# RWKV chain: one prepared matrix per chunk, one product per head, output by tokens

## The chip, the cores and the metric

The kernel is one program on one core of a Trainium2 chip, written in Bass with the Tile framework. The metric is device time in microseconds (us). A core has TensorE (matrix products), VectorE, ScalarE and GpSimd (elementwise work), and SyncE, which issues the DMAs here; the profile calls them PE, DVE, ACT, POOL and SP, and TensorE's weight loads PEld.

## The reference

Two layers over 1024 latent tokens and 128 context tokens, 1024 channels. Layer 1's mixer runs a bidirectional RWKV-7 recurrence (512 channels, 8 heads of 64) beside a bidirectional mLSTM (the other 512). The change is in the recurrence, which for each head and direction carries a 64 x 64 state over the tokens:

```
def step(S, inp):
    r_t, w_t, k_t, v_t, kk_t, a_t = inp
    sa = einsum('bhvk,bhk->bhv', S, -kk_t)
    S = S * w_t[..., None, :] + sa[..., None] * (kk_t * a_t)[..., None, :] + v_t[..., None] * k_t[..., None, :]
    y = einsum('bhvk,bhk->bhv', S, r_t)
    return S, y
```

After the scan the outputs of both directions are added, normalised per head (`head_layer_norm`), and joined with a bonus term and a gate. The last states of the context tokens are outputs too.

## The kernel before

The tokens are columns and the channels partitions everywhere but in the recurrence, which is done in chunks of 64 tokens. A *step* is a pair of heads `p` (four pairs) and an index `i`: for `i` from 0 to 7 the 128-token block `i` forward and block `7 - i` backward, for `i = 8` the context block. A step thus has four units `u` (two directions, two chunks each) and two heads `hh` in the two halves of the partitions. There are 36 steps.

`odd_layer_mixer` sets the order of the work. Its `while` loop is a planner; a turn of it advances the chain of the current step by two stages (`chain_block`), each of at most two preparations by one (`prep`), a finished block by one (`finish`), and hands out pieces of other work by a quota: `R1` pieces a turn while the input projection is being made (`input_pieces`: large products of 384 tokens, L234 to L236), `R2` once the mLSTM runs. A new preparation starts at the earliest `STAG` turns after the last. The framework's scheduler then fixes each engine's order, mixing the pieces finely. Each engine runs its list in order.

`prep` is independent of the state, and has 19 stages. It loads `AG`, `BK` and `vv`; multiplies a chunk with itself (L1119) and masks that into `GB` and the other half of `AG` (L1122, L1123); transposes `BK` into `BT` (L1128); inverts a triangular 64 x 64 matrix per head in half precision, by merging blocks of 1, 2, .. 32 (L1149, L1166, L1171, L1086) and a Newton step (L1197 to L1202); and ends in `Pm` (L1207). `XV` and `UV` hold, for a head, the state or `U` in one half of the partitions and the values in the other.

`chain` depends on the state and is the recurrence from chunk to chunk. For a direction and a chunk it makes five products for each of two heads: `pr` from `AG` and `XV` (L1259), which VectorE copies to `rh`; `pu` from `Pm` and `rh` (L1267), copied to `UV`; `px` from `BT` and `UV` (L1272); and `py` as a sum of two products (L1274, L1275). ScalarE makes `Xw`, the decayed state (L1264); VectorE writes the new state; `py`, by channels, goes into `yo`. `finish` transposes `yo` to tokens for the norm (L1306) and back (L1320).

In the profile a float32 product leaves two MATMUL records, a transpose or a float32r or half-precision product one. `64*128` is the block of the array that a product uses: rows, then columns.

Of the kernel before, what the change touches and what calls it, by code (L numbers as in the profile page):

```python
# [12 lines left out]
F32 = mybir.dt.float32  # L13
# [4 lines left out]
OP = mybir.AluOpType  # L18
# [4 lines left out]
P = 128  # L23
# [28 lines left out]
# arrays of per-channel parameters, and their numbers of columns  # L52
# [11 lines left out]
def trunk_kernel(ctx: ExitStack, tc: tile.TileContext, A, outs, dbg=None, upto=99, odd="rm"):  # L64
    """A: input APs by name; outs: output APs; tokens are columns, channels are partitions."""
# [93 lines left out]
    def mod_ve(l, i0, pool, bank):  # L159
        """512 columns with the products on the vector engine, and only the last sum on the tensor engine."""  # L160
# [28 lines left out]
    def side(gens):  # L189
        """Steps of the generators in turn; a function that does the next n (a fraction: now and then one)."""  # L190
# [38 lines left out]
    def gemm(ps, W, cols, act, nk, start=True, stop=True):  # L229
        """ps += W[:, :, cols]^T act in three passes; act(part, k): the high or the low part of a k tile."""  # L230
# [10 lines left out]
    def rsqrt_small(dst, v, n, pool):  # L241
        """dst = v ** -0.5 on a small tile: a first value from the bits, then three Newton steps."""
# [9 lines left out]
    class Rms:  # L252
        """1 / rms of the tokens of x; the squares are added up tile by tile."""
# [14 lines left out]
        def cols(self, tb):  # L268
            """Tokens on partitions: [128, 3]."""
# [16 lines left out]
        def rows(self, tb, bank=None, r=None):  # L286
            """Repeated over the partitions (in PSUM): [128, 384]."""
# [12 lines left out]
    def norm_coef(l, which, k0=0, n=KT):  # L300
        """norm_w * (1 + scale) per stream: [128, 8, 2], or some of its tiles."""
# [10 lines left out]
    def new_h():  # L312
        """The high and low parts of 1024 channels: h(part, k, tb) is [128, 384]."""
# [35 lines left out]
    def accumulate_x(x, ps, l, which, m, tb):  # L349
        """x[tb][:, m] += gate * ps."""  # L350
# [5 lines left out]
    def mlp(x, l, h, last, add, after, later=()):  # L356
        """x += g2 * (relu(h @ w1)^2 @ w2), 512 hidden channels at a time."""
        with ExitStack() as es:
# [4 lines left out]
            def up(m, n=2.2):  # L363
                """A generator, a token block at a time."""
# [22 lines left out]
            # the first tiles on all but the last block, whose activations come last  # L387
# [21 lines left out]
            # the last hidden channels: a token block after another, half of the weights where the last block's  # L409
            # activations were  # L410
# [12 lines left out]
    def finish(x, tb, rms):  # L423
        """Final norm of a token block. A generator of four steps."""
# [66 lines left out]
            # shift and scale of the first norm  # L491
# [30 lines left out]
    # =========================== layer 0, mixer ===========================  # L522
    def norm(x, l, which):
        """The normalised activations; what takes in a tile of x; what computes a block of tokens."""
# [4 lines left out]
        def block(tb):  # L529
            """A generator of four steps."""  # L530
# [15 lines left out]
    def early(block):  # L546
        """A step of blocks 0 and 1 after each tile of the last block's products."""
        return itertools.chain(block(0), block(1))

    def even_layer_mixer(h, even_u, even_gate, zs, load_y):  # L550
        """Its output, split; what the tiles of channels come to in order."""
        yh = new_h()
        with ExitStack() as es:
# [4 lines left out]
            # block-diagonal gate weights: [128, (dir, which, tile), 128]  # L558
# [5 lines left out]
            # log_a / 4 and log_a / 2 at an open gate  # L564
# [9 lines left out]
            def rglru(j, u, gate):  # L574
# [11 lines left out]
                for d in range(2):  # L586
# [3 lines left out]
                    # sigmoid(x) = (1 + tanh(x / 2)) / 2  # L590
# [1290 lines left out]
```

## Time and profile before

| | before |
|---|---|
| device time, three runs | 3512.77, 3525.55, 3534.02 us (median 3525.55) |
| profiled execution, span | 3541.4 us |
| TensorE, VectorE, ScalarE busy in it | 3362.6, 1993.8, 1476.1 us |
| layer 1's mixer, first to last product | 1303.4 to 2607.4 us |
| TensorE busy there, mean granted clock | 1220.2 us of 1304.0, 0.90 |

The page gives no other time of the profiled execution than its span, from the first to the last instruction. Busy times count an engine's own instructions. A matmul's length includes its way through the array, so that neighbours overlap; what one costs is read from start to start. The granted clock is the share of TensorE's 2.4 GHz that it was given.

### The profile page before, as it was taken

How to read it: one execution, taken by the hardware profiler on the slowest of the kernel's cores; microseconds unless marked ns; L12 is line 12 of the kernel's file. 1: busy time of each engine (PE TensorE's matmuls, PEld its weight loads, DVE VectorE, ACT ScalarE, POOL GpSimd, SP SyncE). 2: the span in 40 equal slices, each digit the busy share in tenths (PEclk: the TensorE clock that was granted, in tenths of full speed). 3: DMA queues.
4: the chain of work that ended last, by engine and by line, in shares of the span. 5: the costliest groups of instructions: out<-in, count | busy, mean ns of one | idle time of the engine just before them, and what ended most of it. 6: DMA issues, size and time to landing. Idle time of an engine off the chain costs nothing. (4 is left out here: it accounts for less than half of the span.)

```text
span 3541.4 us, 57533 instructions
## 1 busy us (share of the span) xinstructions
PE 3362.6 (95%) x22456; PEld 3021.0 (85%) x22456; DVE 1993.8 (56%) x4326; ACT 1476.1 (42%) x3443; POOL 850.2 (24%) x709
## 2 busy tenths in 40 slices
PE   7887999999999998999999999998889999999998
PEld 4766999999999987777777677777789999999998
DVE  6786665555533375676576775647756333333335
ACT  4534332111122255655666566677845122221112
POOL 2232321112111233141151421113313111111112
PEclk9998999999999998888889899999989999999999
DMA  5334412322211125232132322246452111111111
GB/s 207 103 129 155 137 52 92 96 87 92 78 42 42 55 102 156 79 112 73 53 118 83 113 69 82 72 119 170 122 168 63 48 42 42 42 42 42 42 42 73
DMA packets 212978, 313.21 MB, mean 88 GB/s; under 512 B 38034, under 2 KB 154978, under 8 KB 211170
## 3 DMA queue, kind: packets, MB, share of 16 engines
q1 hardware_dynamic: 212706, 309.53, 27.6%
q8 instruction: 177, 2.90, 0.3%
q14 instruction: 95, 0.78, 0.1%
HBM read 250.72 MB, written 58.74 MB: 87 GB/s over the span
## 5 line engine op out<-in xcount | busy, mean ns | idle before, releaser
L234 PE MATMUL mm<-h,w 128*128 128x384 f32 x2552 | 903.6, 355 | 2.1 <-ACT h L503 1.2
L235 PE MATMUL mm<-h,w 128*128 128x384 f32 x2552 | 902.0, 353 | 3.0 <-POOL h L506 1.5
L236 PE MATMUL mm<-h,w 128*128 128x384 f32 x2552 | 900.3, 353 | 2.0 <-POOL w L217 2.0
L217 POOL TENSOR_TENSOR w<-w 128x1024 fp32r<-128x1024 f32 x153 | 373.6, 2442 | 1361.1 <-ACT w L216 1312.5
L216 ACT CAST w<-w 128x1024 fp32r<-128x1024 f32 x211 | 221.2, 1050 | 886.4 <-PE mm L235 769.8
L354 DVE SCALAR_TENSOR_TENSOR x<-mm,mod,x 128x384 f32<-128x384 f32 (+1 forms) x576 | 282.9, 514 | 444.8 <-PE mm L236 418.4
L234 PE MATMUL mm<-uH,w 128*128 128x384 f32 x1536 | 520.3, 339 | 0.0
L235 PE MATMUL mm<-uL,w 128*128 128x384 f32 x1536 | 519.2, 338 | 0.0
L236 PE MATMUL mm<-uH,w 128*128 128x384 f32 x1536 | 519.0, 338 | 0.0
L234 PEld LDWEIGHTS mm<-h,w 128*128 128x128 f32 x2552 | 493.9, 194 | 23.3 <-issue 11.3
L235 PEld LDWEIGHTS mm<-h,w 128*128 128x128 f32 x2552 | 493.6, 193 | 19.2 <-POOL h L506 4.5
L236 PEld LDWEIGHTS mm<-h,w 128*128 128x128 f32 x2552 | 494.4, 194 | 14.5 <-issue 4.5
L374 DVE SCALAR_TENSOR_TENSOR s<-mm,r 128x384 f32<-128x384 f32 x192 | 106.8, 557 | 405.6 <-ACT r L372 405.5
L234 PEld LDWEIGHTS mm<-uH,w 128*128 128x128 f32 x1536 | 288.7, 188 | 2.5 <-issue 2.5
L235 PEld LDWEIGHTS mm<-uL,w 128*128 128x128 f32 x1536 | 288.6, 188 | 0.0
L236 PEld LDWEIGHTS mm<-uH,w 128*128 128x128 f32 x1536 | 288.6, 188 | 0.0
L372 ACT ACTIVATE r<-mm 128x384 f32<-128x384 f32 x192 | 93.5, 488 | 276.9 <-PE mm L236 276.2
L217 DVE TENSOR_TENSOR uL<-s,uH 128x384 fp32r<-128x384 f32 x192 | 150.2, 783 | 87.6 <-ACT uH L216 87.2
L1086 ACT COPY DB<-YQ 64x256 f16<-64x256 f16 x360 | 144.4, 402 | 55.2 <-DVE YQ L1171 36.6
L1171 DVE CAST_PREDICATED YQ<-lm,sm 128x512 f16<-128x512 uint16 x180 | 123.6, 687 | 69.2 <-PE sm L1149 48.1
L1149 PEld LDWEIGHTS <-DB 128*128 128x128 f16 x1728 | 90.2, 101 | 83.2 <-issue 40.5
L216 ACT CAST uH<-s 128x384 fp32r<-128x384 f32 x192 | 98.5, 513 | 143.7 <-DVE s L374 143.5
(378 smaller groups left out, 5312.1 us busy)
## 6 DMA issues: line engine op xcount, KB each, us to landing
w<-in_mlp_w_dram SPq DMA_DIRECT2D x128, 512.0 KB
wmod<-in_w_mod_dram SPq DMA_DIRECT2D x80, 512.0 KB
w<-in_od_w_in_dram SPq DMA_DIRECT2D x31, 512.0 KB
w<-in_od_w_out_dram SPq DMA_DIRECT2D x24, 512.0 KB
zar<-AR SPq DMA_DIRECT2D x24, 384.0 KB
AG<-zar SPq DMA_DIRECT2D x144, 64.0 KB
BK<-zbk SPq DMA_DIRECT2D x72, 128.0 KB
hbig<-zm SPq DMA_DIRECT2D x18, 512.0 KB
```

Source lines behind the costliest of these rows:

```text
L216: sc.copy(Hout, src)
L217: eng.tensor_tensor(Lout, src, Hout.bitcast(F32), op=OP.subtract)
L234: te.matmul(ps, wH[:, k, cols], aH, start=start and k == 0, stop=False)
L235: te.matmul(ps, wH[:, k, cols], aL, start=False, stop=False)
L236: te.matmul(ps, wL[:, k, cols], aH, start=False, stop=stop and k == nk - 1)
L354: ve.scalar_tensor_tensor(xs, ps[:, o], modcol(l, 2 if which == 1 else 5, m, s), xs, op0=OP.mult, op1=OP.add)
L372: sc.activation(r, ps[:, :TB], AF.Relu)
L374: ve.scalar_tensor_tensor(s, ps[:, :TB], 0.0, r, op0=OP.max, op1=OP.mult)
L1086: sc.copy(dst[hr, :, hr], src[hr])
L1149: te.matmul(o[r_, u], lt[r_, u], rt[r_] if rt is i16 else rt[r_, u], start=True, stop=True)
L1171: ve.copy_predicated(YQ.rearrange("p w (d c) n -> p (w d) c n", d=2), lmask(l, 0, 4), pyq.rearrange("p (w c) n -> p w c n", c=2),)
```

## The change

For each unit and head the preparation now makes one 128 x 128 matrix, `EF`, that takes state and values (`XV`) to the new state before its decay and to the chunk's output, together. `prep` gets four more stages (23): it transposes the masked half of `AG` into `AT`, multiplies it with the inverse (`PD`, both heads on a diagonal) into `WT`, multiplies that with `GB` (which now also holds the transposed `BK`) and adds `AG`, in which an identity stands for the state's own part. `AG` becomes two fixed buffers, one for each of the two preparations under way, instead of three in turn.

`chain_block` then has one product per direction and head; VectorE multiplies the state's half with the decay `wend` into the next `XV`, and the other half is the output, already by tokens, in `ys`. Copies through `rh`, `UV`, `Xw` and `BT` go. `finish` needs no transpose before the norm, and four small products per block instead of one transpose behind it. `wend` is stored in the order of the chain; `AR` is stored to DRAM by three DMAs instead of one; the first states are loaded into `XV`. The planner's numbers change.

```
-        STAG = 10
-        R1, R2 = 0.32, 1.6
+        STAG = 11
+        R1, R2 = 0.29, 1.45
 # expand
-                    sy.dma_start(
-                        zar[p][d][:, tb * NC6 : tb * NC6 + NC6, :], AR.rearrange("p c a t -> p c (a t)")
-                    )
+                    sy.dma_start(zar[p][d][HR[1], cs6, :], AR[HR[1]].rearrange("p c a t -> p c (a t)"))
+                    for i in range(2):
+                        sy.dma_start(zar[p][d][HR[0], cs6, (1 - i) * CH : (2 - i) * CH], AR[HR[0], :, i])
 # prep
-            B.AG = mp.tile([P, 2, 4, P], F32, tag="AG", name="AG", bufs=NB)
+            AG = AGs[bank]
...
-            sc.copy(B.BT, pt.rearrange("p (u n) -> p u n", u=4))
+            ptv = pt.rearrange("p (u n) -> p u n", u=4)
+            for hh, hr in enumerate(HR):
+                ho = HR[1 - hh]
+                sc.copy(GB[hr, :, BETA[hh]], ptv[hr, :, hr])
+                sc.copy(AG[ho, :, 5 * hh], ptv[ho, :, hr])
...
+            pt = smps(bank)
+            for u in range(4):
+                te.transpose(pt[:, u * P : u * P + P], AG[:, u, 2:4].rearrange("p w n -> p (w n)"), ident)
+            AT = mp.tile([P, 4, P], F32, tag="AT", name="AT", bufs=1)
+            sc.copy(AT, pt.rearrange("p (u n) -> p u n", u=4))
+            yield
             pq = quads(smps(bank))
             mm2(pq, N1, Q)
-            B.Pm = mp.tile(U4, F32, tag="Pm", name="Pm", bufs=2)
-            ve.tensor_tensor(B.Pm, pq, Q, op=OP.add)
+            for hr in HR:
+                ve.tensor_tensor(PD[hr, :, hr], pq[hr], Q[hr], op=OP.add)
             yield
+            pw = smps(bank)
+            for u in range(4):
+                te.matmul(pw[:, u * P : u * P + P], PD[:, u], AT[:, u], start=True, stop=True)
+            WT = mp.tile([P, 4, P], F32, tag="WT", name="WT", bufs=1)
+            sc.copy(WT, pw.rearrange("p (u n) -> p u n", u=4))
+            yield
+            B.EF = mp.tile([P, 2, 4, P], F32, tag="EF", name="EF", bufs=2)
+            for hh, hr in enumerate(HR):
+                pf = smps(bank)
+                right = cols(GB, hh, EFFECT)
+                for u in range(4):
+                    te.matmul(pf[:, u * P : u * P + P], WT[hr, u], right[hr, u], start=True, stop=True)
+                ve.tensor_tensor(B.EF[:, hh], pf.rearrange("p (u n) -> p u n", u=4), cols(AG, hh, EFFECT), op=OP.add)
+                yield
 # chain_block, for q in range(2), in place of chain
+                pc_ = smps(2 + q)[:, : 4 * CH].rearrange("p (d h v) -> p d h v", d=2, h=2)
+                for d in range(2):
+                    for hh in range(2):
+                        te.matmul(pc_[:, d, hh], B.EF[:, hh, us[d]], B.XV[:, us[d], hh], start=True, stop=True)
+                yield
...
+                        w = wend[hr, p, 2 * i + q].unsqueeze(2).to_broadcast([64, 2, CH])
+                        ve.tensor_tensor(X[hr, :, hh if X.shape[2] > 1 else 0], pc_[hr, :, hh], w, op=OP.mult)
...
+                    if i < 4 or (i == 8 and q == 0):
+                        sc.copy(o, src)
+                    else:
+                        ve.tensor_add(o, o, src)
+                yield
 # finish
-            for q in range(k):
-                te.transpose(pn[:, q * P : q * P + P], fc[:, q], ident)
+            for g in range(2 * k):
+                gs = slice(g * CH, g * CH + CH)
+                for hh, hr in enumerate(HR):
+                    ho = HR[1 - hh]
+                    te.matmul(pn[hr, gs], flat_(fc)[ho, gs], ident[ho, ho], start=True, stop=True)
```

The order of the instructions on TensorE in two places. The names are output <- inputs, behind them the output's size; `sm`, `mm` and `ex` are banks of PSUM, and L numbers are lines of the kernel that the listing is of. First the chain of one chunk in the first half of the mixer, before: `px` and `py` of one direction among the large products of the input projection.

```order
L235 MATMUL mm<-h,w 128x384
L1272 MATMUL sm<-UV,BT 64x64 x2
L1274 MATMUL sm<-AG,XV 64x64
L1275 MATMUL sm<-GB,UV 64x64
L1274 MATMUL sm<-AG,XV 64x64
L1275 MATMUL sm<-GB,UV 64x64
L236 MATMUL mm<-h,w 128x384
```

Now (L1296 is the chain's product, L1163 the chunk with itself, L1198 the inversion):

```order
L1198 LDWEIGHTS DB
L1198 MATMUL sm<-YQ,DB 128x64
L1163 MATMUL sm<-AG,BK 128x128
L1296 MATMUL sm<-XV,EF 128x64 x4
L1163 MATMUL sm<-AG,BK 128x128
L1198 LDWEIGHTS DB
L1198 MATMUL sm<-R,DB 128x64
```

The whole chain of a chunk is four products in a row, and the weights of all four fill the array. Listing by listing, L1259 stands in 167 runs (17 of them with all four products), L1267 in 107 (39), and L1272 with what follows it in 144. Of the new lines L1296 stands in 42 runs that another block shape follows, L1272 (`EF`) in 77, L1357 (`finish`) in 51. In the mixer, places where the next product has another block shape go from 1743 to 906.

Second, the end of the mixer, before: the last chunk's chain, and then the output projection (L1656 to L1658).

```order
L1274 MATMUL sm<-AG,XV 64x64
L1275 MATMUL sm<-GB,UV 64x64
L1274 MATMUL sm<-AG,XV 64x64
L1275 MATMUL sm<-GB,UV 64x64
L1658 MATMUL mm<-h,w 128x384
L1656 MATMUL mm<-h,w 128x384
L1657 MATMUL mm<-h,w 128x384
```

And now (L1263 makes `WT`, L1272 `EF`, L1296 is the chain, L1693 to L1695 the output projection, L1357 is in `finish`):

```order
L1198 MATMUL sm<-YQ,DB 128x64
L1263 MATMUL sm<-AT,PD 128x128 x4
L1272 MATMUL sm<-GB,WT 128x128 x8
L1296 MATMUL sm<-XV,EF 128x64 x8
L1693 MATMUL mm<-h,w 128x384
L1694 MATMUL mm<-h,w 128x384
L1357 MATMUL ex<-ident,f_c 64x64 x4
L1693 MATMUL mm<-h,w 128x384
```

The last step's preparation ends in three groups of products that stand back to back with both chunks of its chain; the last piece of the mLSTM stands some 490 rows ahead of the last chain, where before it stood some 20 rows ahead of it.

## Rows read from the trace of the kernel before

**Rows 1.** The page's busy shares, and its 40 slices: TensorE, then its granted clock.

```profile
PE 3362.6 (95%) x22456; PEld 3021.0 (85%) x22456; DVE 1993.8 (56%) x4326; ACT 1476.1 (42%) x3443; POOL 850.2 (24%) x709
...
PEclk9998999999999998888889899999989999999999
```

**Rows 2.** Windows view: length, busy us (instructions) of five engines, granted clock, DMA share, GB/s.

```profile
2371.80:2607.40 235.60, 201.26 (x1835) 169.87 (x1835) 169.61 (x578) 175.60 (x558) 68.14 (x88) 0.90 0.51 145
1303.40:2607.40 1304.00, 1220.23 (x10358) 967.18 (x10357) 868.69 (x2450) 835.56 (x2398) 341.68 (x397) 0.90 0.34 102
```

**Rows 3.** Waits view, TensorE, 1303 to 2608 us: us in total, times, longest.

```profile
PE sm L1149 <- ACT R L1166: 7.4, 17, 1.1
```

**Rows 4.** Line L1207, thrice: count, ns min/median/max, first to last start; whole, 2130:2345, 2400:2600.

```profile
L1207 DVE TENSOR_TENSOR Pm<-sm,YQ x36: 410/418/426, 1430.4 to 2581.2; 128x256 f32<-128x256 f32 x36
...
L1207 DVE TENSOR_TENSOR Pm<-sm,YQ x9: 417/418/425, 2141.6 to 2343.6; 128x256 f32<-128x256 f32 x9
...
L1207 DVE TENSOR_TENSOR Pm<-sm,YQ x5: 416/418/419, 2404.2 to 2581.2; 128x256 f32<-128x256 f32 x5
```

**Rows 5.** Timeline of TensorE at full clock: start us, length us, records.

```profile
2123.06 0.34 PE L236 MATMUL mm<-h,w 128*128 128x384 f32 x1
2123.24 0.34 PE L234 MATMUL mm<-h,w 128*128 128x384 f32 x1
2123.51 0.93 PE L1119 MATMUL sm<-AG,BK 64*128 64x128 f32 x6
2124.37 0.29 PE L1149 MATMUL sm<-YQ,DB 128*128 128x64 f16 x4
...
2125.55 0.45 PE L1267 MATMUL sm<-rh,Pm 64*64 64x64 f32 x8
2125.93 0.45 PE L234 MATMUL mm<-h,w 128*128 128x384 f32 x1
...
2127.41 0.34 PE L1272 MATMUL sm<-UV,BT 128*64 128x64 f32 x4
2127.57 0.28 PE L1274 MATMUL sm<-AG,XV 128*64 128x64 f32 x2
2127.78 0.33 PE L1275 MATMUL sm<-GB,UV 64*64 64x64 f32 x2
...
2128.55 0.34 PE L1272 MATMUL sm<-UV,BT 128*64 128x64 f32 x4
...
2129.98 0.60 PE L1128 MATMUL sm<-ident,BK 128*128 128x128 f32 x4
2130.33 0.42 PE L236 MATMUL mm<-h,w 128*128 128x384 f32 x1
```

**Rows 6.** The same view: a run of two products of the chain.

```profile
2379.78 0.34 PE L1259 MATMUL sm<-XV,AG 128*64 128x64 f32 x4
2380.04 0.71 PE L1119 MATMUL sm<-AG,BK 64*128 64x128 f32 x4
```

**Rows 7.** The same view: float32 products with 128 columns of weights and two moving.

```profile
1426.47 0.72 PE L939 MATMUL ex<-halves,sq 128*128 128x2 f32 x6
1427.05 0.28 PE L1149 MATMUL sm<-YQ,DB 128*128 128x64 f16 x4
```

**Rows 8.** Windows view around a fall of the clock.

```profile
1605.20:1610.70 5.50, 5.50 (x62) 4.19 (x62) 3.03 (x14) 3.99 (x12) 0.64 (x1) 1.00 0.00 0
1610.70:1631.20 20.50, 20.50 (x123) 16.05 (x125) 7.91 (x28) 8.61 (x26) 0.82 (x2) 0.50 0.16 46
```

**Rows 9.** Timeline of TensorE at half clock.

```profile
1614.34 0.52 PE L236 MATMUL mm<-h,w 128*128 128x384 f32 x1
1614.65 0.52 PE L234 MATMUL mm<-h,w 128*128 128x384 f32 x1
```

**Rows 10.** Groups of instructions, VectorE and ScalarE, 1303.4 to 2607.4 us: count, busy us, mean ns.

```profile
L1122 DVE TENSOR_TENSOR GB<-sm,gm 64x512 f32<-64x512 f32 x72 | 49.5, 687 | 28.3 <-PE sm L1119 27.3
...
L1264 ACT ACTIVATE Xw<-XV,wend 64x64 f32<-64x64 f32 x288 | 99.3, 345 | 29.9 <-DVE XV L1282 19.2 <-DVE X L1278 3.9 <-POOL wend L987 1.5
```

More of the change, by code (lines that the diff above doesn't have):

```diff
@@ L954, in ck, with chain_order @@
             return t.rearrange("p (c t) -> p c t", t=CH)
+        def chain_order(d, a, b):
+            if d == 0:
+                return [(a, b, a)]
+            out = []
+            for s0, n in STREAMS:
+                lo, hi = max(a, s0 // CH), min(b, (s0 + n) // CH)
+                if lo < hi:
+                    out.append((lo, hi, (2 * s0 + n) // CH - hi))
+            return out
         def expand(p):
@@ L1081, in rwkv @@
             DB.append(t)
+        PD = mp.tile([P, 4, P], F32, tag="PD", name="PD")
+        gp.memset(PD, 0.0)
+        AGs = []
+        for i in range(2):
+            t = mp.tile([P, 4, 6, CH], F32, tag=f"AG{i}", name="AG")
+            for hh, hr in enumerate(HR):
+                ve.tensor_copy(t[hr, :, 5 * hh], ident[hr, hr].unsqueeze(1).to_broadcast([64, 4, CH]))
+            AGs.append(t)
+        PRODUCTS, EFFECT, ALPHA, BETA = ((1, 3), (0, 2)), ((0, 2), (1, 3)), (2, 0), (0, 2)
         state = {}
@@ L1093, in u22, with cols, block_of @@
             return t.rearrange("p (d c) n -> p d c n", d=2)
+        def cols(t, hh, which):
+            a, b = which[hh]
+            k = t.shape[2] // 2 * hh if t.shape[2] == 6 else 0
+            return t[:, :, k + a : k + b].rearrange("p u w n -> p u (w n)")
         Bs = {}
+        def block_of(p, i):
+            if (p, i) not in Bs:
+                B = Bs[p, i] = Ctx()
+                B.XV = mp.tile([P, 4, 2, CH], F32, tag="XV", name="XV", bufs=3)
+            return Bs[p, i]
         def prep(n, p, i):
-            B = Bs[p, i] = Ctx()
+            B = block_of(p, i)
             bank = n % 2
             tb = blocks(i)
-            B.AG = mp.tile([P, 2, 4, P], F32, tag="AG", name="AG", bufs=NB)
+            AG = AGs[bank]
             BK = mp.tile([P, 4, P], F32, tag="BK", name="BK", bufs=1)
@@ L1138, in prep @@
             Y, Q = YQ[:, 0], YQ[:, 1]
-            diag(N1, GB[:, :, 0:CH])
+            lower = [GB[:, :, k] for k in ALPHA]
+            diag(N1, lambda hr: lower[HR.index(hr)][hr])
             ve.tensor_copy(Q, ib)
@@ L1216, in start_pair @@
                 ve.tensor_copy(rkb[hr, hr], pc("rw_rk", p)[hr].to_broadcast([64, 64]))
-            X = []
-            for d in range(2):
-                X.append(mp.tile([P, CH], F32, tag="X", name="X", bufs=4))
-                sy.dma_start(X[d], A["state_rwkv"][d, p])
-            state["X"] = X
         def chain_block(p, i):
-            B = Bs.pop((p, i))
+            B = block_of(p, i)
             if i == 0:
@@ L1227, in chain_block @@
             tb = blocks(i)
-            X, seen, yo = state["X"], state["seen"], state["yo"]
-            for d in range(2):
-                u = 2 * d + d
-                for hh, hr in enumerate(HR):
-                    o = B.XV[hr, u, hh, :]
-                    if i < 8:
-                        sc.copy(o, X[d][hr])
-                    else:
-                        gp.memset(o, 0.0)
-            for q in range(2):
-                gs = []
-                for d in range(2):
-                    cc = 1 - q if d else q
-                    c = 2 * tb[d] + cc
-                    gs.append(chain(B, p, d, cc, c, q == 1, yo, c not in seen, X))
-                    seen.add(c)
-                for _ in range(4):
-                    for g in gs:
-                        next(g)
-                    yield
@@ new lines, in chain_block @@
+            ys = state["ys"]
+            for q in range(2):
+                us = (1, 2) if q else (0, 3)
+                pc_ = smps(2 + q)[:, : 4 * CH].rearrange("p (d h v) -> p d h v", d=2, h=2)
+                for d in range(2):
+                    for hh in range(2):
+                        te.matmul(pc_[:, d, hh], B.EF[:, hh, us[d]], B.XV[:, us[d], hh], start=True, stop=True)
+                yield
+                X = None
+                if q == 0:
+                    X = B.XV[:, 1:3]
+                elif i < 7:
+                    X = block_of(p, i + 1).XV[:, 0::3]
+                elif i == 8:
+                    X = mp.tile([P, 2, 1, CH], F32, tag="X", name="X", bufs=2)
+                if X is not None:
+                    for hh, hr in enumerate(HR):
+                        w = wend[hr, p, 2 * i + q].unsqueeze(2).to_broadcast([64, 2, CH])
+                        ve.tensor_tensor(X[hr, :, hh if X.shape[2] > 1 else 0], pc_[hr, :, hh], w, op=OP.mult)
+                if i == 8 and q:
+                    for d in range(2):
+                        sy.dma_start(outs["new_rwkv"][d, p], X[:, d, 0])
+                c0, c1 = 2 * tb[0] + q, 2 * tb[1] + 1 - q
+                lo, hi = sorted((c0, c1))
+                for hh in range(2):
+                    ho = HR[1 - hh]
+                    o = ys[ho, lo : hi + 1 : hi - lo]
+                    src = pc_[ho, :, hh] if c0 < c1 else pc_[ho, ::-1, hh]
+                    if i < 4 or (i == 8 and q == 0):
+                        sc.copy(o, src)
+                    else:
+                        ve.tensor_add(o, o, src)
+                yield
```

113 lines of the change are left out of this document (39 added, 74 removed).

## The prediction

> **What bounds the kernel now.** I read the page's busy shares and clock first. TensorE is busy 95% of the span, and the clock granted to it is full nearly everywhere except in the slices of layer 1's mixer [rows 1]. The change touches that mixer alone, so the windows view comes next: from 1303.4 to 2607.4 us, 1304.0 us in all, TensorE is busy 1220.2 us, VectorE 868.7 and ScalarE 835.6, and the mean clock is 0.90 [rows 2]. TensorE has only two levels, 2.4 and 1.2 GHz, so a mean of 0.90 means a fifth of the time, about 260 us, at half clock. The waits view has nothing to set against this: TensorE idles 1304.0 - 1220.2 = 84 us, and the largest single cause is 7.4 us [rows 3]. So the mixer ends when TensorE has worked through its list, and two things set how long that takes: what the products cost, and how often they run at half clock.
>
> **Pace.** The last product of the preparation (`Pm`, once a step) stands 36 times between 1430.4 and 2581.2 us [rows 4]: 1150.8 / 35 = 32.9 us a step. A preparation has 19 stages and its end is noticed one turn of the planner's loop later; two run at a time, so a step is 10 turns of 3.29 us. Counting the whole loop gives 375 turns.
>
> **What goes.** The timeline at full clock shows what five small products cost [rows 5]. A big product follows the next after 0.18 us (2123.06 to 2123.24), but after 0.27 when the next works on another block shape: 0.09 us for a change of shape. A run of four products (eight records, since a float32 product leaves two) takes 2125.55 to 2125.93 = 0.38, its leaving included; a shorter run 2379.78 to 2380.04 = 0.26 [rows 6]. The last three products of the chain change shape at nearly every product: 2127.41 to 2128.55 = 1.14 us for one direction.
> In the order of before the first product of the chain (L1259) stands in 167 runs, 17 of them of four; the second (L1267) in 107, 39 of them of four. So: 17 x 0.38 + 150 x 0.26 = 45; 39 x 0.38 + 68 x 0.26 = 33; 144 x 1.14 = 164; and 167 + 107 + 144 = 418 entries at 0.09 = 38. The chain costs **280 us** of TensorE.
>
> **What comes**, all by the same rows.
> - One product per head, chunk and direction: 288, 576 records, with 128 columns of float32 weights and 64 moving columns. The trace has no such product. The nearest is L939: the same weights with only 2 moving columns still take 1426.47 to 1427.05 = 0.58 for six records, the last five at about 0.112, against 0.38 for eight (0.047 each) with 64 columns of weights [rows 5, 7]. So the weights set the price, and I take 0.112: 65 us, and 84 shape changes, 8. At 0.047 it would be 27.
> - `PD` times `AT`: 288 records of the same weights, 32 us. The transposes into `AT`: 144, four of which take 2129.98 to 2130.33 = 0.35, 13 us [rows 5].
> - The products into `EF`: 576 records of 64 rows and 128 columns, the shape of L1119, which takes 0.86 for six with its leaving (2123.51 to 2124.37); at 0.112 a record and 0.09 for each of 154 changes, 78 us.
> - `finish`: 72 transposes at 0.09 go (6), 144 small float32 products come: 288 records at 0.047 and some 100 changes, 23. Net 17.
> Together 65 + 8 + 32 + 13 + 78 + 17 = 213. **TensorE: 213 - 280 = -67 us**; -105 if the chain's new product costs 0.047 a record.
> If the changes of shape were free, the old chain would cost 2880 records at 0.047 = 135 us, and the change would add 213 - 135 = 78. The rows speak against it: one direction's twelve last records take 1.14 us, not 0.56 [rows 5]. The Trainium skill's TensorEngine Tiling (Array Packing), Theoretical Speedup, has it that way: products that are small in one size run up to twofold side by side. The trace has that only for neighbours of one shape, which are rare here.
>
> **What lies beside it.** VectorE loses `rh`, half of `UV` and four state updates a step, and gains two sums into `EF`, each the size of L1122's 0.687 us [rows 10]; that balances. ScalarE loses 288 `Xw` of 0.345 us [rows 10], the copies of `X` and all of `UV`, and gains `AT`, `WT` and two pairs of copies: some 100 us less. Neither ends the mixer today, so I cost both at nothing; TensorE's list is their cover, and if it shrinks further VectorE, at 869 of then 1190 us, comes nearest. SyncE gets 56 more issues, also nothing. `AG` now has two fixed buffers, held until `EF` is made, so that a load waits for that; TensorE wants it two turns later. Bounds: nothing, or a turn per step, 36 x 3.29 = 118 us; I take nothing, because no DMA stands near the top of the waits [rows 3].
>
> **The clock.** From 1605.2 to 1610.7 us TensorE is busy for all of the 5.50 us at full clock, and the next 20.5 us are granted at half [rows 8]. What it did before the fall was a string of chain products and other small ones that use half or a quarter of the array, with one big product among them; no idle time. At half clock a big product takes 1614.34 to 1614.65 = 0.31 instead of 0.18 [rows 5, 9]. So the 260 us would be 260 x 0.18 / 0.31 = 151 at full clock: up to **109 us** to be had. The change replaces 2880 records of half and quarter blocks mostly by whole blocks and by 64 x 128, in less time. I take two thirds back, -73; the bounds are 0 and -109.
>
> **Waits.** A preparation gets 23 stages, 24 turns for two steps, so a step takes 12 turns and the loop 446. Each turn has less TensorE work in which to hide the way over VectorE or ScalarE and back. The planner hands out other work at 0.29 x 12 = 3.5 pieces a step (3.2 before) and then 1.45 x 12 = 17.4 (16), so it runs out some three steps before the end, where TensorE will wait most. I add 25 us, between 0 and a doubling of today's 84.
> **Sum:** -67 - 73 + 25 = -115 us against the profiled span of 3541.4, thus 3426; the median of the runs, 3525.55, is 15.9 below that span, which gives **3410 us**.
>
> **The rivals.**
> 1. The clock stays as it is, because preparation, not the chain, makes it fall. For: the half-precision products of the inversion are small too and stay. Then -67 + 25 = -42: 3484. Chance 0.22.
> 2. Better on all counts: 0.047 a record, all of the clock, no new waits: -105 - 109 = -214: 3312. Chance 0.07.
> 3. Slower: the turn becomes the bound. Place: every turn of the mixer, a preparation's stage to VectorE or ScalarE and back. It decides where a turn cannot be shorter than 375 x 3.29 / 446 = 2.77 us; at 2.9 the loop takes 446 x 2.9 - 375 x 3.29 = +60: 3586. For it: between 2404.2 and 2581.2 us a step takes 44.3, 4.4 a turn, and TensorE idles most there, 235.6 - 201.3 = 34 us [rows 2, 4]. Against it: from 2141.6 to 2343.6, at full clock, eight steps take 25.3 each, 2.5 a turn, with more work per turn than will be left [rows 4]. Chance 0.06.
> 4. The clock falls more often, because TensorE idles more. In the trace it fell without idle time [rows 8], so this stands on little. If the share at half clock went from a fifth to three tenths, that is 130 x (1 - 0.18 / 0.31) = +55, and -67 + 25 + 55 = +13: 3539. Chance 0.05. TensorE: Matmul & The Clock Gate, Part 1, in the Trainium skill, has this rule: activity releases the throttle and an idle stretch brings it back; the trace has a fall that it does not explain.
> 5. The changes of shape cost nothing, because TensorE would have waited there anyway: +78 + 25 = +103: 3629. Chance 0.02.
>
> **How the numbers follow.** The forecast has 0.58. It spreads from 3350 to 3450 by the bounds of clock and waits, rival 1 from 3450 to 3495 by its waits. Leaving out rivals 2 to 5 (0.20) gives the range 3345 to 3495. A measurement here tells half a per cent, 18 us: faster is the forecast and rivals 1 and 2, 0.87; same rival 4, 0.05; slower rivals 3 and 5, 0.08.
>
> **What would show it.** Right: the mixer's window near 1190 us, mean clock 0.96 or more in it, about 1000 fewer TensorE records, the chain's product at 0.11 a record back to back, steps of 28 to 30 us in the middle. Wrong: a mean clock of 0.90 (rival 1); TensorE busy under 90% of the mixer with turns of 2.8 us or more (rival 3); `AG` loads among TensorE's waits; or a mixer whose end, without other work, takes over 100 us.

## The result, and the profile after

The changed kernel takes 3547.09 us (median; the kernel before, beside it, 3527.06): a ratio of 1.006, with a 95% interval of 1.0032 to 1.0087. It is slower by a little, where 3410 was predicted and 3345 to 3495 was the range. The profiled spans are 3543.4 and 3541.4 us, so the traces show the same thing: nothing gained, a trifle lost. One kernel's executions differ, and with them the clock granted over the whole program: in the 109 executions of before for which the runs of this case give it, the clock lies between 0.951 and 0.967 and the time between 3504 and 3548 us, in the main the shorter the higher the clock. The traced execution of before, with 0.952, is one of those with a low clock.

The page of after, TensorE's busy time and its granted clock (compare [rows 1]): 1080 records fewer, 50 us less busy, and a hole in the clock near the end of the mixer.

```profile
PE 3312.5 (93%) x21376; PEld 3034.2 (86%) x21376; DVE 2002.5 (57%) x4070; ACT 1385.9 (39%) x2919; POOL 847.5 (24%) x706
...
PEclk9998999999999998988989899999579999999999
```

I cut the mixer into four stages: the **start**, to the first product of the chain; the **main** stage, to the first product of the mLSTM; the **mLSTM**, to its last product; and the **end**, where only the recurrence and the output are left. The windows view of after, these four and the whole (columns as in [rows 2]):

```profile
1302.30:1454.70 152.40, 115.17 (x643) 93.39 (x642) 82.65 (x165) 64.50 (x131) 38.49 (x42) 0.84 0.42 114
1454.70:2316.80 862.10, 810.23 (x6601) 676.45 (x6600) 600.07 (x1447) 495.14 (x1199) 229.77 (x261) 0.92 0.33 92
2316.80:2520.70 203.90, 177.50 (x1571) 156.62 (x1568) 149.37 (x433) 149.94 (x456) 61.57 (x78) 0.91 0.52 146
2520.70:2607.10 86.40, 65.76 (x464) 52.61 (x462) 46.11 (x151) 35.65 (x90) 8.33 (x12) 0.58 0.26 82
1302.30:2607.10 1304.80, 1168.66 (x9272) 979.07 (x9271) 878.20 (x2195) 745.24 (x1874) 338.16 (x393) 0.89 0.36 102
```

The same four of before:

```profile
1303.40:1424.30 120.90, 104.73 (x570) 86.78 (x568) 69.23 (x134) 59.31 (x120) 38.69 (x41) 0.89 0.46 141
1424.30:2371.80 947.50, 914.24 (x7957) 710.54 (x7955) 629.85 (x1740) 600.65 (x1722) 234.86 (x268) 0.91 0.28 86
2371.80:2591.30 219.50, 189.82 (x1764) 160.66 (x1764) 158.69 (x541) 169.16 (x545) 68.14 (x88) 0.90 0.50 141
2591.30:2607.40 16.10, 11.44 (x72) 9.21 (x71) 10.92 (x37) 6.44 (x14) 0.00 (x0) 0.82 0.59 193
```

To see what a stage should have cost, each TensorE record is given a price: the usual distance, at full clock, from its start to the next record's, by the shapes of both, from the trace of before (the chain's new product at the 0.112 us found below). The sum is TensorE's **list**, an estimate; what a stage takes beyond it is waits and half clock, the **surplus**. In us, time / list / surplus:

| | start | main | mLSTM | end | mixer |
|---|---|---|---|---|---|
| before | 121 / 95 / 26 | 948 / 806 / 142 | 220 / 164 / 56 | 16 / 9 / 7 | 1304 / 1075 / 229 |
| after | 152 / 100 / 52 | 862 / 724 / 138 | 204 / 149 / 55 | 86 / 38 / 48 | 1305 / 1011 / 294 |

The list is shorter by 64. (That hangs on what is taken for usual: by the mean of the distances without idle time it is shorter by 50, by their median by 86.) The surplus is longer by 65: 41 at the end, 26 at the start, and next to nothing off in the main stage, where the clock was to give it back.

The chain's new product at full clock, in the timeline of after (start us, length us): six records take 2133.13 to 2133.71 = 0.58, as the six of [rows 7] do, and eight take 2134.53 to 2135.37 = 0.84.

```profile
2133.13 0.78 PE L1296 MATMUL sm<-XV,EF 128*128 128x64 f32 x6
2133.71 0.42 PE L234 MATMUL mm<-h,w 128*128 128x384 f32 x1
...
2134.53 1.00 PE L1296 MATMUL sm<-XV,EF 128*128 128x64 f32 x8
2135.37 0.28 PE L1198 MATMUL sm<-R,DB 128*128 128x64 f16 x4
```

The end: line L1258 finishes the inverse, twice a step, in all the mixer and after 2521 us (columns as in [rows 4]). Three steps end there, without other work; from the first of them to the last are 57.3 us, 28.6 a step.

```profile
L1258 DVE TENSOR_TENSOR PD<-sm,YQ x72: 408/422/429, 1442.4 to 2587.1; 64x256 f32<-64x256 f32 x72
...
L1258 DVE TENSOR_TENSOR PD<-sm,YQ x6: 409/422/428, 2529.8 to 2587.1; 64x256 f32<-64x256 f32 x6
```

The start, in the waits view of TensorE from 1302 to 1455 us (us in total, times, longest). A load of `AG` shows up, 5.8 us; in before no load is waited for here. The other two lines are of products that make the recurrence's inputs, ahead of the first preparation.

```profile
PE ex L949 <- DVE rb L946: 7.7, 3, 5.6
PE ex L981 <- ACT ld L988: 6.8, 3, 4.3
PE sm L1163 <- DMA AG<-zar: 5.8, 1, 5.8
```

### The profile page after: what moved, and what is told of

Same layout as the page of the kernel before. It is cut to its first block, busy times and chain, and to the rows that moved or that the text cites. A ratio compares the mean times of both kernels' runs of the same rounds, so it can differ in the third digit from the quotient of the medians.

```text
span 3543.4 us, 54607 instructions
## 1 busy us (share of the span) xinstructions
PE 3312.5 (93%) x21376; PEld 3034.2 (86%) x21376; DVE 2002.5 (57%) x4070; ACT 1385.9 (39%) x2919; POOL 847.5 (24%) x706
## 5 line engine op out<-in xcount | busy, mean ns | idle before, releaser
L1198 PEld LDWEIGHTS <-DB 128*128 128x128 f16 x1728 | 93.6, 104 | 90.0 <-issue 50.3
```

Of the source, the lines that this page charges most:

```text
L1198: te.matmul(o[r_, u], lt[r_, u], rt[r_] if rt is i16 else rt[r_, u], start=True, stop=True)
```

## The experiments

Eighteen kernels, numbered in the order in which they ran. Ratios are to the kernel before, run beside them; brackets are 95% intervals.

**1 and 2: the quota.** The first theory was that the 0.29 and 1.45 pieces a turn, at 12 turns a step, hand out the other work too early. Kernel 1 hands out as much a step as before did; kernel 2 slows only the mLSTM.

```
# 1
-        R1, R2 = 0.29, 1.45
+        R1, R2 = 0.27, 1.36
# 2
+        R1, R2 = 0.29, 1.0
```

> The changed kernel with R1, R2 = 0.27, 1.36 in place of 0.29, 1.45: the pieces of other work last for 446 turns instead of 413. Theory A (handing out): the changed kernel's mixer is as long as before because other work is handed out per turn, a step has 12 turns instead of 10, and so the work runs out some three steps early; from the last piece of the mLSTM to the mixer's end it takes 86 us at a mean clock of 0.58, against 16 us before. A expects that stretch at 15 to 35 us, the mixer at 1235 to 1260 instead of 1305, and 3480 to 3500 us in all. Theory B (turns): a turn is bound by the way over VectorE or ScalarE and back, so spreading the same pieces only moves the waiting: mixer 1295 to 1310, in all 3535 to 3555.

> The changed kernel with R1, R2 = 0.29, 1.0: the input projection as fast as in the changed kernel, the mLSTM slower, to the end. A expects the end covered as in e1_quota and, since TensorE waits most while the mLSTM runs, a little more: mixer 1225 to 1255, in all 3470 to 3495 us. B expects no change: 3535 to 3555.

Kernel 1: 3501.38 us, 0.9926 [0.9898, 0.9953]. Kernel 2: 3529.64, 1.0022 [1.0001, 1.0044]. Main stage, end and whole mixer of kernel 1, windows view:

```profile
1459.00:2333.40 874.40, 828.01 (x6940) 680.73 (x6938) 614.88 (x1496) 517.50 (x1267) 231.91 (x265) 0.95 0.33 93
...
2540.20:2558.10 17.90, 11.95 (x81) 9.39 (x81) 12.35 (x37) 8.27 (x17) 1.66 (x2) 0.87 0.65 213
1307.00:2558.10 1251.10, 1136.65 (x9270) 944.01 (x9270) 864.18 (x2194) 741.83 (x1872) 338.42 (x393) 0.93 0.38 106
```

The surplus of the end falls from 48 to 7 us and the whole mixer by 54; two numbers decide whether this change loses 0.6% or gains 0.7%. The mixer and the end are as theory A expected, and the total lies just over its range. Kernel 2 met neither expectation: it has a shorter end (39.2 us), but its input pieces are used up just as early as in the changed kernel, at the 28th step.

**3: the same fault in the kernel before.** Its quota raised in the same measure.

```
-        R1, R2 = 0.32, 1.6
+        R1, R2 = 0.348, 1.74
```

> The kernel before with R1, R2 = 0.348, 1.74, which is what the changed kernel hands out per step (3.48 and 17.4) over 10 turns. A expects the same uncovered end without the change: 50 to 85 us from the last piece of the mLSTM to the mixer's end instead of 16, some 30 to 55 us more in all (3555 to 3580). B expects little, since the turns are the same: within 10 us of before.

3542.03 us, 1.0063 [1.0033, 1.0092]: the loss of the changed kernel, without the changed arithmetic. The 20 us lie between the two expectations, 10 and 30; the uncovered end is there, and longer than expected. Its end, windows view:

```profile
2522.10:2617.70 95.60, 81.04 (x612) 58.86 (x611) 52.27 (x193) 46.80 (x146) 9.14 (x16) 0.61 0.27 86
```

**4: is the end slow because of its clock?** Two unneeded products of 256 columns a turn keep TensorE busy once the other work is used up.

```
+            if not fills:
+                pd = exps()
+                for _ in range(2):
+                    te.matmul(pd[:, :256], ident, par[:, :256], start=True, stop=True)
```

> The changed kernel with two float32 products of 256 columns a turn, into a bank that nobody reads, once the other work is used up: some 70 products, about 30 us of TensorE at full clock, and no new dependence. If the end is long because TensorE runs at half clock there, the clock rises over 0.85 in the stretch and it takes 65 to 80 us instead of 86 in spite of the added work. If it is long because of the ways over VectorE and ScalarE and back, the clock rises too, but the stretch stays at 85 us or more.

3546.31 us, 1.0055 [1.0032, 1.0078]. Its end:

```profile
2519.00:2613.40 94.40, 84.41 (x611) 66.42 (x611) 48.84 (x161) 37.78 (x95) 8.63 (x12) 0.87 0.24 72
```

The clock there goes from 0.58 to 0.87, and the end is no shorter: by what was expected, the ways over VectorE and ScalarE set it. But the critical view of these 94.4 us (the chain of work that ended last, by line; L848 makes the unneeded products) says that the kernel doesn't part the two causes:

```profile
by line: PE ex L848 37.0%; PE sm L1276 6.9%; PE sm L1202 6.5%; PE sm L1300 5.4%; PE sm L1267 5.1%; PE ex L1361 4.5%; PE sm L1167 3.9%; ACT XV L1238 3.3%; issue 2.7%; DVE DB L1251 1.8%; ACT DB L1115 1.7%; PE mm L1697 1.5%; PE mm L1698 1.5%;
```

The unneeded products are themselves 35 us of that chain: they stand in front of the needed ones, and a step takes 34 us instead of 28.6. In the changed kernel the same chain, in the last 50.5 us of the end, is 26.8 us of TensorE, 23.6 of them at half clock, and 19.7 of VectorE and ScalarE. So both have a part in the 28.6 us, and how much the clock alone costs there is not shown.

**5, 6 and 7: the start, and fewer stages.** Kernel 5 is kernel 1 with more pieces until the first chain; kernel 6 has 21 stages (both `EF` sums in one, `AT` beside the Newton step); kernel 7 is both.

```
# 5 and 7 (R1, R2 = 0.25, 1.36 and 0.28, 1.36)
+            quota += R2 if started[1] else R1 if nchain or chain else 0.6
# 6 (STAG = 10; R1, R2 = 0.3, 1.36)
-            pt = smps(bank)
+            pt = exps()
...
-            yield
...
-                pf = smps(bank)
+                pf = exps() if hh else smps(bank)
...
-                yield
+            yield
```

> e1_quota with the other work handed out at 0.6 pieces a turn until the first chain starts, and R1 = 0.25 after it (R2 = 1.36), so that the pieces last as long. In the changed kernel the stretch from the mixer's first product to the first chain takes 152 us instead of 121, at a clock of 0.84, with TensorE idle for 37 of them. Theory A (cover): the first preparation's own way through its stages is what this stretch lasts, and more other work fits beside it for nothing: the stretch stays at 150 to 158 us, the rest of the mixer loses 15 to 30, the mixer is 1220 to 1240 and the whole 3475 to 3490 us. Theory B: TensorE's list is what it lasts, so the stretch grows by what is added (some 25 us) and nothing is gained: mixer 1245 to 1260, in all 3495 to 3510.

> The changed kernel with two of the four new stages of the preparation taken back: AT is transposed in the stage of PD, and both sums into EF are made in one stage, in two banks. 21 stages, a step in 11 turns; STAG 10, R1, R2 = 0.3, 1.36, which make the other work last as in e1_quota. If the number of stages is what the first preparation costs, the stretch to the first chain falls from 152 to 143 to 147 us, the mixer from 1251 (e1_quota) to 1235 to 1245, in all 3485 to 3495. If the way through the same products is what counts, nothing changes: 1248 to 1258 and 3495 to 3505.

> e6_fewer_stages with 0.6 pieces a turn until the first chain, and R1 = 0.28 after it. Theory A (cover) expects the sum of both: mixer 1210 to 1230, in all 3465 to 3480. Theory B expects no more than e6_fewer_stages.

Kernel 5: 3529.13 us, 1.0006 [0.9981, 1.0032]; 6: 3536.18, 1.0023 [1.0001, 1.0045]; 7: 3533.29, 0.9999 [0.998, 1.0019]. None helps: 5 and 6 miss every range given for them, and 7 is no better than 6, as its theory B has it. In kernel 5 the start's list grows by 35 us (134 against 99 in kernel 1) and its time by 32.5 (184.5 against 152.0): the pieces do not fall into the waits, they come on top, and are then missing at the mLSTM, which takes 243 us instead of 207. Kernel 6's mixer is 44 us longer than that of kernel 1, and not where it was expected to change: with two stages fewer the start takes 175 us instead of 152, with 143 more records in it, 81 of them of the input projection; the mLSTM takes 223 us. The main stage is as long as in kernel 1 (876 and 874 us), though at a clock of 0.92 (143 us at half clock against 85).

**8: the twelve turns without the arithmetic.** The kernel before, with four empty stages behind its preparation, at the numbers of kernel 1.

```
-        STAG = 10
-        R1, R2 = 0.32, 1.6
+        STAG = 11
+        R1, R2 = 0.27, 1.36
...
-            yield
+            for _ in range(5):
+                yield
```

> The kernel before with four empty stages at the end of the preparation: 23 stages and 12 turns a step, as in the changed kernel, with STAG 11 and R1, R2 = 0.27, 1.36, which make the other work last to the end. The same products as before. If the pace in turns is what costs, this is slower than before by 20 to 60 us (3545 to 3580) and what the change itself gives is that much more than e1_quota shows against before. If not, it is within 10 us of before (3515 to 3535).

3503.2 us, 0.9922 [0.9894, 0.9949], below both ranges expected; start, main stage and mixer:

```profile
1300.90:1422.10 121.20, 103.84 (x557) 84.64 (x555) 69.97 (x134) 58.94 (x119) 37.96 (x41) 0.90 0.45 138
1422.10:2322.60 900.50, 868.69 (x7957) 678.20 (x7956) 632.01 (x1738) 596.31 (x1713) 232.57 (x268) 0.95 0.30 91
...
1300.90:2555.90 1255.00, 1176.03 (x10370) 934.51 (x10369) 868.95 (x2447) 832.70 (x2395) 339.71 (x397) 0.93 0.35 106
```

That is all of kernel 1's gain, within the intervals. At this pace kernel 8's list is 1071 us and kernel 1's 1012, 59 less; the surplus is 184 and 239, 55 more (27 at the start, 24 in the main stage). The new arithmetic is worth nothing here: what it takes off the list comes back as surplus. The start is as long as in before, so four more stages alone don't lengthen it.

In the traces the clock of the main stage goes from 0.91 to 0.95 with the old products in it. But these are one execution each, and kernel 8's is one of its shortest (3486.2 us). Over all executions the clock of the whole program hardly differs:

| kernel | clock, traced execution | clock, median of its executions | before beside it, median |
|---|---|---|---|
| 1, changed, 12 turns | 0.960 | 0.9585 | 0.962 |
| 8, before, 12 turns | 0.965 | 0.960 | 0.957 |
| 9, before, 14 turns | 0.966 | 0.9655 | 0.959 |
| 10, changed, 14 turns | 0.969 | 0.9645 | 0.959 |
| 17, changed, 14 turns, no empty stages | 0.949 | 0.9555 | 0.959 |

At half clock a large product takes 0.31 us instead of 0.18 [rows 5, 9], so 42% of the time at half clock is lost; 0.001 of the clock is some 7 us at half clock and by that estimate 3 us of time. So the clock accounts for some 9 of kernel 8's 28 us, for 19 of 51 and 16 of 57 us in kernels 9 and 10 below, and for nothing in kernel 1 (for 6 of 27 in kernel 12, which is kernel 1 again). What the rest of the gain is, no run shows.

**9, 10, 11 and 12: fourteen turns, and the empty stages elsewhere.** Kernels 9 (before) and 10 (changed) get four empty stages more behind the preparation. Kernel 11 is kernel 8 with its four empty stages inside the inversion. Kernel 12 is kernel 1 again.

```
# 9 and 10
+        STAG = 13
+        R1, R2 = 0.23, 1.17
# 9: range(9) in place of range(5); 10, behind EF:
+            for _ in range(4):
+                yield
# 11, at the end of an inner level
                     diag(QB, Q)
+                    yield
                 yield
```

> The kernel before with eight empty stages behind its preparation, so that a step has 14 turns, at the same pieces a step (R1, R2 = 0.23, 1.17). Theory A (thinner turns: the fewer small products stand in a turn, the more big ones stand between them, and the less often the clock falls): the gain of 12 turns goes on, mean clock of the mixer 0.94 or more, 3480 to 3500 us. Theory B (twelve turns merely fit the waits: what the chain gains is lost as soon as a turn is shorter than the way over VectorE or ScalarE and back): 3510 to 3540, steps of 31 us or more in the first half at full clock. Theory C (the twelve-turn gain is the phase that two preparations happen to have): no order in the numbers, 3500 to 3540.

> The changed kernel with four empty stages behind EF, so that a step has 14 turns, at the same pieces a step (R1, R2 = 0.23, 1.17). Theory A: 3480 to 3500 us, a mean clock of 0.94 or more in the mixer. Theory B: the longer preparation (23 working stages) makes waits first here, so later than the kernel before with 14 turns, 3515 to 3545. Theory C: 3500 to 3540, without order.

> The kernel before with 12 turns a step as in the eighth experiment, but the four empty stages stand inside the inversion (one behind each of its first four levels) instead of behind the preparation. Theory A: the turns are as thin as in the eighth experiment, so 3495 to 3515 us and the same clock (0.93). Theory C (it was where the gap stands): nearer to the kernel before, 3520 to 3540.

> The changed kernel with R1, R2 = 0.27, 1.36 once more, beside the kernels above. All theories: 3495 to 3510 us. If the changed arithmetic is worth nothing at this pace, it lies within 10 us of the kernel before with 12 turns, in either place of the empty stages, if these two keep their gain.

| kernel | us | ratio |
|---|---|---|
| 9, before, 14 turns | 3479.09 | 0.9859 [0.9823, 0.9896] |
| 10, changed, 14 turns | 3472.41 | 0.9831 [0.9797, 0.9864] |
| 11, before, 12 turns, spread | 3551.15 | 1.005 [1.0014, 1.0087] |
| 12, changed, 12 turns | 3502.52 | 0.9915 [0.9881, 0.9948] |

Kernel 10 is the fastest of all. Its list is 63 us below kernel 9's and its surplus 44 above (217 and 173), so perhaps a little of the new arithmetic is left; the intervals overlap. Kernels 9 and 10 lie under the range of theory A, by 1 and 8 us. Kernel 11, with the turns as thin as in kernel 8, gains nothing, and is later than either theory expected: theory A falls there.

**13 to 18: more turns without empty stages.** In the changed kernel (16: the one before) `STAG` alone was raised.

```
# 13, 14, 15, 16
+        STAG = 13  # R1, R2 = 0.23, 1.17
+        STAG = 17  # 0.18, 0.91
+        STAG = 23  # 0.135, 0.683
+        STAG = 19  # 0.162, 0.82
# 17, 18
+        STAG = 14  # 0.231, 1.18
+        STAG = 17  # 0.192, 0.985
```

> The changed kernel with a preparation begun every 14 turns (STAG 13; R1, R2 = 0.23, 1.17, the same pieces a step), without the empty stages of the tenth experiment: a prepared block then waits for its chain instead of an empty stage. Theory A (fewer small products in a turn): as the tenth, 3460 to 3485 us. Theory C (the gain came with where the empty stages stood): nearer to the twelve-turn kernel, 3490 to 3520.

> The same with 18 turns a step (STAG 17; R1, R2 = 0.18, 0.91): two preparations stand in the same turn in only 5 or 6 of 18. Theory A: the clock gains once more, mean 0.96 or more in the mixer, 3440 to 3470 us. Theory B (a turn gets too short for the ways over VectorE and ScalarE): the loop has 24 + 36 x 18 = 672 turns, at 1.9 us each 1277, so 3500 or more, at a good clock. Theory C: no order, 3470 to 3530.

> The same with 24 turns a step (STAG 23; R1, R2 = 0.135, 0.683): no two preparations ever stand in the same turn. 24 + 36 x 24 = 888 turns, 1.35 us each if the mixer took 1200. Theory A: best or as good as 18 turns, 3430 to 3470. Theory B: 3550 or more, since a stage to another engine and back took some 1.5 to 2 us in the stretches without other work. Theory C: no order.

> The kernel before with 20 turns a step (STAG 19; R1, R2 = 0.162, 0.82), one preparation at a time, no other edit. Theory A: 3450 to 3480 us, clock of the mixer 0.95 or more. Theory B: 20 + 36 x 20 = 740 turns, 3500 or more at a good clock. If the changed arithmetic is worth what the list of TensorE says (64 us) once the clock is not in the way, the changed kernel at 18 or 24 turns beats this one by 20 us or more; if nothing, they lie within 10.

> The thirteenth to sixteenth kernels ran 13, 17, 23 and 19 turns a step (a start may follow after STAG turns, not STAG + 1) at quotas that handed out only 134 to 141 of the 178 pieces by the last chain; the rest stood behind the mixer, so they say nothing of the turns. Here: the changed kernel, a preparation begun every 14 turns exactly (STAG 14), no empty stages, quota fitted (178 pieces by the last chain, counted from the loop; R1, R2 = 0.231, 1.18). Theory A (thinner turns raise the clock): as the tenth, 3460 to 3490 us. Theory C (the empty stages, and with them the place of the chain against the next preparation, did it): 3500 to 3535.

> The changed kernel with 17 turns a step (STAG 17), no empty stages, quota fitted (177 pieces by the last chain; R1, R2 = 0.192, 0.985). Theory A: as good as 14 turns or better, 3440 to 3480 us. Theory B (a turn of under 2 us is shorter than a stage's way over another engine and back): 622 turns at 2.0 to 2.1 us, 3490 to 3550, at a mean clock of 0.94 or more in the mixer. Theory C: 3490 to 3535, with a clock of 0.92 or less.

Kernels 13 to 16 gave 1.0021, 1.0109, 1.016 and 1.0202, but they settle nothing. I had taken a step for one turn longer than it is, so that the mLSTM was not finished when the recurrence was, and stood alone behind it for 40 to 56 us. With the quota mended, 17 takes 3517.83 us, 0.9964 [0.9934, 0.9994], and 18 takes 3539.6, 1.0029 [1.0005, 1.0052]. 17 is in the range of theory C and 18 is 5 us over it, both with a clock of 0.90 in the mixer. Kernel 17 has kernel 10's fourteen turns and, within a per cent, its pieces a step, and 45 us more. Main stage of 10, then of 17:

```profile
1454.60:2303.70 849.10, 801.83 (x6925) 664.31 (x6924) 614.10 (x1492) 515.08 (x1260) 230.29 (x265) 0.98 0.34 95
```

```profile
1444.10:2357.70 913.60, 859.34 (x7017) 708.33 (x7011) 626.79 (x1512) 519.80 (x1274) 233.76 (x265) 0.91 0.31 88
```

Most of the 64.5 us between these two traces is the clock, 0.98 and 0.91: 41 us at half clock in kernel 10, 160 in kernel 17, by the estimate above 50 us of time. The traces overstate it: 10's is the execution with its highest clock, 17's one with nearly its lowest. But it isn't all the luck of one execution: over the whole program the granted clock lay at 0.961 to 0.969 in four executions of 10 and at 0.948 to 0.961 in ten of 17. By the medians it accounts for some 27 of the 45 us.

**What is settled and what stays open.** Settled: the quota made the end (1, 3), and the gain of the better pace is not the arithmetic's (8). Open: how the end's 28.6 us a step divide between the clock and the ways over VectorE and ScalarE (4); what part of the change makes the start longer (its working stages, the fixed buffers of `AG` or the three stores of `AR`; no kernel parts them); and what the better pace gains, of which the clock is the smaller part. It isn't the number of turns (11 and 17 have as many as 8 and 10), nor a finer mixture: kernel 10's main stage has 28 stretches of over 3 us from one large product to the next and kernel 17's has 31, about as many, but 4 of the former and 8 of the latter hold a fall of the clock. What 1, 8, 9 and 10 have in common, and 11, 17 and 18 have not, is a chain that starts in the turn in which the next preparation but one does, with any empty stages behind the preparation. But the kernel before and kernels 5 and 6 have that too, without the gain, so it is at most a part of the reason, and no run isolates it.

## Why the prediction was wrong

**The list of TensorE: right.** Predicted -67, found -64 by the list above (-50 to -86 by other readings of it); the chain's product was taken at 0.112 a record and has that price; some 1000 records were to go, 1080 went. ScalarE was to lose some 100 us and lost 90 (835.6 to 745.2); VectorE was to balance, 868.7 to 878.2.

**The clock: the step that failed.** The step says that the change "replaces 2880 records of half and quarter blocks mostly by whole blocks", and takes two thirds of 109 us back. It read one fall, [rows 8], and took the kind of product for its cause. But the time at half clock grew: in the traces from 253 to 291 us in the mixer, by the 42% an estimated +16 us where -73 was forecast. In the main stage it fell, from 178 to 133 us; start and end added 20 and 67. And all six executions of after, with a clock of 0.944 to 0.948 over the whole program, lie below all 109 of before. The 109 us to be had were read from an execution of before with 0.952; the median of before is 0.959, some 50 us less at half clock, so there was less to be had in most executions. This is a fall in after; the timeline of TensorE ahead of it (in brackets the idle time just before a group, and who ended it):

```profile
1997.73 0.42 PE L236 MATMUL mm<-h,w 128*128 128x384 f32 x1
1998.62 0.28 PE L1198 MATMUL sm<-R,DB 128*128 128x64 f16 x4 [0.47 <-ACT R L1215]
1998.83 0.31 PE L1198 MATMUL sm<-YQ,R 64*64 64x64 f16 x8
2000.00 0.28 PE L1198 MATMUL sm<-YQ,DB 128*128 128x64 f16 x4 [0.85 <-DVE YQ L1220]
2001.26 0.28 PE L1198 MATMUL sm<-R,DB 128*128 128x64 f16 x4 [0.98 <-ACT R L1215]
2001.46 0.31 PE L1198 MATMUL sm<-YQ,R 64*64 64x64 f16 x8
```

and the windows view of the same stretch and of the one behind it:

```profile
1997.73:2002.10 4.37, 2.06 (x36) 1.61 (x33) 3.58 (x22) 2.88 (x8) 0.00 (x0) 1.00 0.55 156
2002.10:2019.20 17.10, 13.38 (x96) 10.41 (x95) 12.24 (x25) 9.41 (x25) 5.70 (x7) 0.50 0.30 93
```

One large product, then stages of the inversion with TensorE waiting between them for ScalarE and VectorE, then half clock. Taken over the main stage of after, TensorE spent 12% of the 4 us ahead of its 15 falls on large products and 44% on gaps beyond the price list; its averages at full clock are 40% and 17%. In before it is 10% and 29% ahead of 18 falls, with averages of 38% and 17%. (Four us is a stretch that I chose for reading.) So the falls stand where large products are missing, and the removed products left a wait there, not a large product. That this is what makes the clock fall is argued; no run isolates it. TensorE: Matmul & The Clock Gate in the Trainium skill, section A second HAM failure mode: psum-queue depth-cycling, tells of another kernel in which short idle times between groups of products were frequent enough to make the clock go back and forth; these rows agree with that, while [rows 8] has a fall without idle time.

**The waits: right in part of the place, mis-sized.** The step took +25 between 0 and 84, and named the end, three steps without other work. TensorE's idle time in the mixer went from 84 to 136 us, +52: 16 of them at the end, 21 at the start, 19 in the main stage, 3 less in the mLSTM. With half clock the surplus of start and end is +67. The end was named but not priced: three steps without other work took 86 us for a list of 38. Instead a share of today's waits was taken for it. The start wasn't seen at all (121 to 152 us); kernel 8's start shows that the number of stages is not the reason. So -64 of list, +16 of clock and +52 of waits stand in place of -67, -73 and +25; they add up to +4, and the mixer shows +1.
"I take nothing" for the `AG` loads holds but for 7.3 us, 5.8 of them that one wait at the start.

**The rivals.** Rival 1, the clock stays as it is, has a part of the mechanism: its sign, a mean clock of 0.90, is met by 0.89, and the clock gave nothing back; but its waits are too small, and its 3484 is out. Rival 3 comes nearest by its sign: TensorE is busy 89.6% of the mixer, and its turn of 2.9 us is there on paper (1304.8 / 446 = 2.93). Its mechanism is not, since kernel 10 has 520 turns in 1223.3 us, 2.35 each. Rival 4 is nearest with its 3539 us, and right in that the time at half clock grew where TensorE idles more, at the start and the end. But there are fewer falls (26 in the mixer, where before has 31), and its sum is close partly by luck: 55 us for the clock where the traces show 16, and 25 us for the waits where they show 52. Rival 2 is out by the price of the chain's product, and rival 5 by the time, and by TensorE's busy time, which fell by 50 us.

## What to carry to other kernels

A change that alters the number of stages alters every number that is counted per stage: work out at which step each kind of other work runs out, before and after, and price what is left alone there with its waits, not by its list. When a change of arithmetic comes with a change of pace, run the old arithmetic at the new pace before crediting either; here the old arithmetic with four empty stages behind its preparation had the whole gain, and four more gave the two kernels 1.4 and 1.7%. Products taken off TensorE are worth their price only where other work moves up into their place. And a clock that differs between executions of one kernel must be compared over all of them: two traces alone would have put most of kernel 8's gain down to the clock.

## What I had not expected of the hardware

The granted clock can depend on the rhythm of a program and not only on its products: two kernels of the same products and, within a per cent, the same pieces a step had medians of 0.9645 and 0.9555 over the whole program (0.98 and 0.91 in the main stage of the traced executions, 41 and 160 us at half clock), and differ only in four empty stages and in how far apart preparations may start.
One and the same kernel, before, had 0.951 to 0.967 in 109 executions, and its time in the main followed the clock, 3504 to 3548 us.
Unneeded products brought the clock of the end from 0.58 to 0.87 and gained nothing: 35 of its 94.4 us, on the chain that ended last, were those products themselves.
